# Stick-breaking attention by adjacent heads in separate PSUM banks, and expert weights laid out in runs of four rows

## The chip, the cores and the metric

The kernel runs on one core of a Trainium2 chip. The metric is the device time of one execution in microseconds (us); every execution starts with all weights in HBM, and 425 MB are read from there in the course of it. The core's engines work side by side, each through its own list of instructions in order: TensorE (PE), VectorE (DVE), ScalarE (ACT), GpSimd (POOL), and SyncE (SP), whose queue issues nearly all transfers. They wait for each other by semaphores.

## The reference

A sequence of 256 tokens of width 1024 goes through a first block of two layers (feed-forward, a mixer with three branches, feed-forward) and a second block (a gated delta rule, attention in a sliding window, a mixture of experts). Two parts matter here. The first is a branch of the mixer, stick-breaking attention with 16 heads of 64 features; `strict` lets a query see only earlier keys:

```python
def _stick_breaking(qc, kc, vc):          # per block of 128 queries
    z = jnp.einsum('bqhd,bkhd->bhqk', qblk, k).astype(jnp.float32) * scale
    strict = kpos[None, :] < qp[:, None]
    log_stay = jnp.where(strict, jax.nn.log_sigmoid(-z), 0.0)
    after = lax.cumsum(log_stay, axis=3, reverse=True) - log_stay
    a = jnp.where(strict, jnp.exp(jax.nn.log_sigmoid(z) + after), 0.0)
    return jnp.einsum('bhqk,bkhd->bqhd', a.astype(v.dtype), v)
```

The second is the mixture of 32 experts, each with a gate and an up matrix of 1024x256 and a down matrix of 256x1024:

```python
    for e in range(N_EXPERTS):
        hid = jax.nn.silu(t @ w_gate[e]) * (t @ w_up[e])
        out = out + combine[:, e:e + 1] * (hid @ w_down[e]).astype(jnp.float32)
```

## The kernel before

Weights are streamed. A tile of 512 KB is loaded on SP's queue (`raw`, four buffers), split into a rounded half `hi` by ACT (L255) and a rest `lo` by DVE (L256), and used by PE in three passes (L250 to L252, or L293, L294 and L296 with the tokens on the partitions). The rest of the mixer is written as generators, and after each weight tile `execute` advances every active one by a step. So PE's list has attention work between the matmuls of weight tiles, in an order that is fixed when the program is built.

Stick-breaking is one such generator, `stick`. `pipe` runs eight units through three stages; in each round it calls s2 of the unit before, then s1 of the newest, then s3 of the one two back (order 1, 0, 2), and then lets three weight tiles go by.

- s1 computes scores. A unit has two heads. Keys lie on the partitions, queries on the columns. Bank A holds keys 0 to 127 against all 256 queries for both heads (two times 256 columns), bank B keys 128 to 255 against queries 128 to 255 (two times 128). A product contracts 64 features, so it uses 64 of the array's 128 rows. In the kernel before both heads of a unit lie on the same half of the partitions (`p`, by `t % 2`), and the mask is added on PE, as a product of the identity and a bf16 mask (L974, L981). ACT takes Abs, Exp and Ln (L985 to L990), DVE makes softplus and log-sigmoid from that (L992, L993) and splits the softplus (`sph` at L995, `spl` at L996).
- s2 forms the running sums by products with a triangular matrix (L1004 for B, L1007 for A, and L1009 for B's part of A); DVE adds them (L1011), ACT takes Exp (L1012).
- s3 multiplies by the values (L1026, L1027). The output has 64 features of a head on the partitions; here both heads of a unit go to the same half of them.

These matmuls have fp32 operands; each of them leaves two records in the trace. `bank` gives one of five PSUM banks (L107) and `sc` a scratch tile of a pool.

The experts run in 16 pairs and one more unit for tokens that overflow. `hidden` multiplies a pair's tokens by gate and up (L1983), with the two experts on the two halves of the output's partitions, in one bank; `down` multiplies by w_down (L2025), `scatter` puts tokens back (L2038). `expert_gu` loads gate and up: two tiles of 1 MB, each with four of the eight blocks of rows, by four transfers of 512 KB on SP (L1784). Partition p takes rows 8p to 8p+7. The tiles come from a pool of 14 buffers. `expert_d` loads w_down in two tiles (L1798) into the pool of five that `lo` uses. SP issues them in order, and each waits for its buffer and for an earlier transfer.

Of the kernel before, what the change touches and what calls it, by code (L numbers as in the profile page):

```python
# [7 lines left out]
F32 = mybir.dt.float32  # L8
F32R = mybir.dt.float32r
BF16 = mybir.dt.bfloat16  # L10
I32 = mybir.dt.int32
AF = mybir.ActivationFunctionType
ALU = mybir.AluOpType
# [4 lines left out]
S = 256  # L18
NB = 2
KD = 8  # L20
# [69 lines left out]
class Net:  # L90
# [873 lines left out]
    def stick(self, L):  # L964
        nc = self.nc
        nu, none = self.NU[:, 0:128], self.NU[:, 128:129].to_broadcast([128, 128])
        P = {}
        flat = lambda a: a.rearrange("p a b -> p (a b)")

        def s1(t):  # L970
            qT, kT = L["qc"], L["kc"]
            p = slice(64 * (t % 2), 64 * (t % 2) + 64)
            A, B = self.bank([128, 2, S]), self.bank([128, 2, 128])
            nc.tensor.matmul(B, self.identb, self.m_str.rearrange("p (o n) -> p o n", o=1).to_broadcast([128, 2, 128]), start=True, stop=False)  # L974
            for i in range(2):
                r = 2 * (t // 2) + i
                nc.tensor.matmul(B[:, i, :], kT[p, r, 128:256], qT[p, r, 128:256], start=False, stop=i == 1)
            for i in range(2):
                r = 2 * (t // 2) + i
                nc.tensor.matmul(A[:, i, :], kT[p, r, 0:128], qT[p, r, :], start=i == 0, stop=False)  # L980
            nc.tensor.matmul(A[:, :, 0:128], self.identb, self.m_str.rearrange("p (o n) -> p o n", o=1).to_broadcast([128, 2, 128]), start=False, stop=True)  # L981
            for nm, z in (("B", flat(B)), ("A", flat(A))):
                n = z.shape[1]
                e = self.sc([128, n], F32, "ze")
                nc.scalar.activation(e, z, AF.Abs)  # L985
                if t == 0 and nm == "B":

                    self.tc.keep_in_program_order(nc.scalar.preload_act_table_set("natural_log_exp_and_others"))
                nc.scalar.activation(e, e, AF.Exp, scale=-1.0)
                nc.scalar.activation(e, e, AF.Ln, bias=1.0)  # L990
                sp = self.sc([128, n], F32, "sp", True)
                nc.vector.scalar_tensor_tensor(sp, z, 0.0, e, op0=ALU.max, op1=ALU.add)  # L992
                nc.vector.scalar_tensor_tensor(e, z, 0.0, e, op0=ALU.min, op1=ALU.subtract)  # L993
                hi, lo = self.sc([128, n], F32R, "sph"), self.sc([128, n], F32R, "spl")
                nc.vector.tensor_copy(hi, sp)  # L995
                nc.vector.tensor_tensor(lo, sp, hi.bitcast(F32), op=ALU.subtract)  # L996
                P[nm, t] = (e, hi, lo)

        def s2(t):
            eB, *spB = P["B", t]  # L1000
            eA, *spA = P["A", t]
            B = self.bank([128, 256])
            for i, s in enumerate(spB):
                nc.tensor.matmul(B, nu, s, start=i == 0, stop=i == 1)  # L1004
            A = self.bank([128, 2, S])
            for i, s in enumerate(spA):
                nc.tensor.matmul(flat(A), nu, s, start=i == 0, stop=False)  # L1007
            for i, s in enumerate(spB):
                nc.tensor.matmul(A[:, :, 128:256], none, s.rearrange("p (a b) -> p a b", a=2), start=False, stop=i == 1)  # L1009
            for e, x in ((eB, B), (eA, flat(A))):  # L1010
                nc.vector.tensor_tensor(e, e, x, op=ALU.add)  # L1011
                nc.scalar.activation(e, e, AF.Exp)  # L1012

        def s3(t):
            if t == 0:
                L["stick"] = (self.t8([128, KD, S], F32R, "och"), self.t8([128, KD, S], F32R, "ocl"))
            if t % 2 == 0:
                P["o"] = self.bank([128, 2, S])
            v = L["vc"]
            aB, aA = P.pop(("B", t))[0], P.pop(("A", t))[0]  # L1020
            p = slice(64 * (t % 2), 64 * (t % 2) + 64)
            for i in range(2):
                h = 4 * (t // 2) + t % 2 + 2 * i
                o = P["o"][p, i, :]
                hc = slice(h * 64, h * 64 + 64)
                nc.tensor.matmul(o, v[:, 0, hc], aA[:, i * 256:(i + 1) * 256], start=True, stop=False)  # L1026
                nc.tensor.matmul(o[:, 128:256], v[:, 1, hc], aB[:, i * 128:(i + 1) * 128], start=False, stop=True)  # L1027
            if t % 2 == 1:
                oh, ol = L["stick"]
                r = t - 1  # L1030
                self.split(oh[:, r:r + 2, :], ol[:, r:r + 2, :], P["o"])

        yield from self.pipe(8, (s1, s2, s3), 3, order=(1, 0, 2),
                             ready=lambda t: all((n, min(t, 7) // 2) in L["done"] for n in ("qc", "kc")) and (t < 2 or ("vc", min(t - 2, 7) // 4) in L["done"]))

# [742 lines left out]
    def expert_gu(self, e):  # L1778
        nc, I = self.nc, self.I
        ts = []  # L1780
        for j in range(2):
            t = self.big.tile([128, 2048], F32, name="wgu", tag="b8").rearrange("p (k s n) -> p k s n", k=4, s=2)
            for s, nm in ((0, "w_gate_2"), (1, "w_up_2")):
                nc.sync.dma_start(t[:, :, s, :], I[nm][0, e].rearrange("(p k) n -> p k n", k=KD)[:, 4 * j:4 * j + 4, :])  # L1784
            ts.append(t)
        return lambda k: [(slice(0, 512), ts[k // 4][:, k % 4, :, :].rearrange("p s n -> p (s n)"))]

    def expert_d(self, e, big=False, later=None):
        src = self.I["w_down_2"][0, e].rearrange("(p k) n -> p k n", k=2)
# [515 lines left out]
```

## Time and profile before

| | |
|---|---|
| runs | 2177.97, 2170.87, 2175.85 us; median 2175.85 |
| profiled execution | 2174.99 us, span 2173.1 us |
| PE busy | 2113.4 us, 97% of the span |
| DVE busy | 1342.6 us, 62% |
| ACT busy | 994.7 us, 46% |
| POOL busy | 83.3 us, 4% |
| HBM read | 425.50 MB, 196 GB/s over the span |

The span is the time from the first to the last instruction of one profiled execution, and busy means that an engine had an instruction under way. Stick-breaking runs from about 250 to 350 us in layer 0 and from about 1090 to 1190 us in layer 1; the experts run from about 1890 us to the end. The page's rows show one execution; the median above is over others.

### The profile page before, as it was taken

Reading aid. Unit: us, or ns where it says so; the run is one execution under the profiler, and the core shown is the slowest. Engines: PE = TensorE matmul, PEld = TensorE weight load, DVE = VectorE, ACT = ScalarE, POOL = GpSimd, SP = SyncE. Lnnn points to the kernel's source line nnn. Section 1 sums busy time; section 2 is a strip of 40 time slices with the busy share of each in tenths; the row PEclk is TensorE's granted clock in tenths of the full one; section 3 lists DMA queues with packets and bytes.
Section 4 is the critical chain, followed back from the end, with each engine's and each line's share of the span. In section 5 each row is a group of like instructions: output and inputs, shape, how many; then the busy total and the mean of one; then the engine's idle time right before and its main releaser. Section 6 shows DMA issues by size and latency. Waiting matters only on the chain.

```text
span 2173.1 us, 35223 instructions
## 1 busy us (share of the span) xinstructions
PE 2113.4 (97%) x14059; PEld 1805.8 (83%) x14059; DVE 1342.6 (62%) x2289; ACT 994.7 (46%) x1671; POOL 83.3 (4%) x73
## 2 busy tenths in 40 slices
PE   8999999999999999999999999999999999798998
PEld 8997978899999988998888889998997888544543
DVE  5556567966676567666677884676555885622232
ACT  5443564765444443444465665544443654211111
POOL 0000000100000000000000010000000111101000
PEclk9999999999999999999999999999999999899999
DMA  7575543455467786887543454465675423799996
GB/s 237 179 213 178 167 115 116 149 156 153 144 193 236 231 274 209 267 266 266 168 131 106 135 161 150 147 187 171 185 224 155 142 81 119 261 347 332 354 344 248
DMA packets 316983, 428.91 MB, mean 197 GB/s; under 512 B 20782, under 2 KB 262672, under 8 KB 315792
## 3 DMA queue, kind: packets, MB, share of 16 engines
q1 hardware_dynamic: 316384, 423.48, 62.3%
q0 software_dynamic: 432, 3.15, 0.3%
q8 instruction: 112, 1.84, 0.3%
q14 instruction: 55, 0.45, 0.1%
HBM read 425.50 MB, written 1.07 MB: 196 GB/s over the span
## 4 chain that ended last, share of the span: by engine, by line
PE 85%; DVE 7%; DMA 4%; ACT 2%; issue 1%; POOL 0%; SPq 0%; ACTq 0%; DVEq 0%; POOLq 0%
PE ps L250 14%; PE ps L252 14%; PE ps L251 14%; PE ps L1983 5%; PE y L293 4%; PE y L294 4%; PE ps L293 3%; PE y L296 3%; PE ps L296 3%; PE ps L294 3%; PE ps L2025 3%; DMA raw<-in_w_ada_dram 2%; DVE lo L256 2%; PE y L2038 1%; PE ps L2130 1%; PE y L282 1%
## 5 line engine op out<-in xcount | busy, mean ns | idle before, releaser
L256 DVE TENSOR_TENSOR lo<-raw,hi 128x1024 fp32r<-128x1024 f32 (+1 forms) x556 | 661.2, 1194 | 437.8 <-ACT hi L255 436.5
L255 ACT CAST hi<-raw 128x1024 fp32r<-128x1024 f32 (+1 forms) x556 | 569.3, 1029 | 697.9 <-PE ps L251 245.4
L250 PE MATMUL ps<-xh,hi 128*128 128x256 f32 (+1 forms) x2232 | 635.3, 285 | 0.0
L252 PE MATMUL ps<-xh,lo 128*128 128x256 f32 (+1 forms) x2232 | 632.0, 283 | 2.2 <-DVE lo L256 2.2
L251 PE MATMUL ps<-xl,hi 128*128 128x256 f32 (+1 forms) x2232 | 631.5, 283 | 0.0
L252 PEld LDWEIGHTS ps<-xh,lo 128*128 128x128 f32 (+1 forms) x2232 | 425.6, 191 | 3.0 <-DVE lo L256 2.4
L250 PEld LDWEIGHTS ps<-xh,hi 128*128 128x128 f32 (+1 forms) x2232 | 425.8, 191 | 2.4 <-issue 1.6
L251 PEld LDWEIGHTS ps<-xl,hi 128*128 128x128 f32 (+1 forms) x2232 | 425.8, 191 | 0.7
L293 PE MATMUL ps<-hi,xh 128*128 128x512 f32 (+1 forms) x368 | 145.8, 397 | 1.2 <-ACT xh L255 0.7
L296 PE MATMUL ps<-hi,xl 128*128 128x512 f32 (+1 forms) x368 | 143.9, 391 | 0.3
L294 PE MATMUL ps<-lo,xh 128*128 128x512 f32 (+1 forms) x368 | 143.7, 391 | 0.0
L293 PE MATMUL y<-hi,hh 128*128 128x512 f32 x352 | 137.5, 391 | 0.0
L294 PE MATMUL y<-lo,hh 128*128 128x512 f32 x352 | 137.2, 390 | 0.2
L1983 PE MATMUL ps<-wgu,hi 128*64 128x512 f32 x512 | 123.9, 598 | 0.0
L296 PE MATMUL y<-hi,hl 128*128 128x512 f32 x352 | 104.5, 389 | 0.0
L1983 PEld LDWEIGHTS ps<-wgu,hi 128*64 128x64 f32 x512 | 42.3, 138 | 70.1 <-issue 67.7
L1124 DVE SCALAR_TENSOR_TENSOR macc<-raw,cols,macc 128x1024 f32<-128x1024 f32 x42 | 53.9, 1282 | 51.7 <-DMA raw<-in_w_ada_dram 51.6
L293 PEld LDWEIGHTS ps<-hi,xh 128*128 128x128 f32 x368 | 69.7, 189 | 17.9 <-issue 2.0
L296 PEld LDWEIGHTS ps<-hi,xl 128*128 128x128 f32 x368 | 69.6, 189 | 16.4 <-DVE xl L256 2.3
L294 PEld LDWEIGHTS ps<-lo,xh 128*128 128x128 f32 x368 | 69.7, 189 | 13.1
L294 PEld LDWEIGHTS y<-lo,hh 128*128 128x128 f32 x352 | 66.1, 188 | 14.4 <-DVE lo L256 1.1
L293 PEld LDWEIGHTS y<-hi,hh 128*128 128x128 f32 x352 | 66.1, 188 | 14.2 <-issue 0.8
(601 smaller groups left out, 3207.8 us busy)
## 6 DMA issues: line engine op xcount, KB each, us to landing
raw<-in_w_mix_in_dram SPq DMA_DIRECT2D x184, 512.0 KB, 3.6
raw<-in_ffn_w_in_dram SPq DMA_DIRECT2D x176, 512.0 KB, 4.6
raw<-in_ffn_w_out_dram SPq DMA_DIRECT2D x88, 512.0 KB, 4.3
wgu<-in_w_gate_dram SPq DMA_DIRECT2D x64, 512.0 KB, 9.2
wgu<-in_w_up_dram SPq DMA_DIRECT2D x64, 512.0 KB, 9.5
lo<-in_w_down_dram SPq DMA_DIRECT2D x54, 512.0 KB, 8.3
raw<-in_w_branch_dram SPq DMA_DIRECT2D x48, 512.0 KB, 3.4
raw<-in_w_ada_dram SPq DMA_DIRECT2D x48, 512.0 KB, 5.0
```

Of the source, the lines that this page charges most:

```text
L250: mm(out, ah, bh, start=start, stop=False)
L251: mm(out, ah, bl, start=False, stop=False)
L252: mm(out, al, bh, start=False, stop=stop)
L255: self.nc.scalar.copy(hi, src)
L256: self.nc.vector.tensor_tensor(lo, src, hi.bitcast(F32), op=ALU.subtract)
L282: self.nc.tensor.transpose(pt[:, k, :], src[:, k * 128:(k + 1) * 128], self.ident)
L293: mm(y, ah[:, t], wh[:, c], start=start, stop=False)
L294: mm(y, ah[:, t], wl[:, c], start=False, stop=False)
L296: mm(y, al[:, t], wh[:, c], start=False, stop=stop)
L1124: nc.vector.scalar_tensor_tensor(acc, raw, c, acc, op0=ALU.mult, op1=ALU.add)
L1983: mm(gu[64 * e:64 * e + 64, c], u["x"](k)[:, 64 * e:64 * e + 64], w, start=k == 0 and i == 0, stop=k == KD - 1 and i == len(ws[0]) - 1)
L2025: mm(y[64 * e:64 * e + 64, :], u["hT"][:, k, 64 * e:64 * e + 64], wd[k][:, c], start=k == 0, stop=k == 1)
```

## The change

In `stick` a unit now has heads 2t and 2t+1, which lie on the two halves of the partitions of feature block t. Each head has a bank of its own, `Z[i]`, with A's scores in columns 0 to 255 (`cA`) and B's in 256 to 383 (`cB`), and the four score products alternate between the heads (L979). The mask is added by DVE in PSUM, once for each head (L984). Abs is taken once for each head and part; the loading of ACT's table follows it. A goes before B from there on, and DVE's softplus and log-sigmoid (L997, L998) are done for each head apart. In s3 the two heads go to the two halves of the output's partitions, products alternating (L1029, L1031). s2 is as before, at L1009 (B), L1012 (A), L1014 (B into A) and L1016.

In `expert_gu` the four rows of a matrix that a partition takes in one transfer now lie beside each other in the tile, so that the transfer is 128x1024 rather than 128x4x256; the operand of `hidden` is then two runs of 256 columns. `expert_d` is as before, at L1802, and the product with w_down at L2029.

```diff
@@ -966,35 +966,40 @@
         nu, none = self.NU[:, 0:128], self.NU[:, 128:129].to_broadcast([128, 128])
         P = {}
         flat = lambda a: a.rearrange("p a b -> p (a b)")
+        halves = [slice(64 * i, 64 * i + 64) for i in range(2)]
+        cA, cB = slice(0, 256), slice(256, 384)
+        strict = self.m_str.rearrange("p (o n) -> p o n", o=1).to_broadcast([128, 2, 128])
         def s1(t):
             qT, kT = L["qc"], L["kc"]
-            p = slice(64 * (t % 2), 64 * (t % 2) + 64)
-            A, B = self.bank([128, 2, S]), self.bank([128, 2, 128])
-            nc.tensor.matmul(B, self.identb, self.m_str.rearrange("p (o n) -> p o n", o=1).to_broadcast([128, 2, 128]), start=True, stop=False)
+            Z = [self.bank([128, 512]) for _ in range(2)]
+            for c, k, q in ((cA, slice(0, 128), slice(0, 256)), (cB, slice(128, 256), slice(128, 256))):
+                for i, p in enumerate(halves):
+                    nc.tensor.matmul(Z[i][:, c], kT[p, t, k], qT[p, t, q], start=True, stop=True)
+            e = {"A": self.sc([128, 2, S], F32, "ze"), "B": self.sc([128, 2, 128], F32, "ze")}
             for i in range(2):
-                r = 2 * (t // 2) + i
-                nc.tensor.matmul(B[:, i, :], kT[p, r, 128:256], qT[p, r, 128:256], start=False, stop=i == 1)
-            for i in range(2):
-                r = 2 * (t // 2) + i
-                nc.tensor.matmul(A[:, i, :], kT[p, r, 0:128], qT[p, r, :], start=i == 0, stop=False)
-            nc.tensor.matmul(A[:, :, 0:128], self.identb, self.m_str.rearrange("p (o n) -> p o n", o=1).to_broadcast([128, 2, 128]), start=False, stop=True)
-            for nm, z in (("B", flat(B)), ("A", flat(A))):
-                n = z.shape[1]
-                e = self.sc([128, n], F32, "ze")
-                nc.scalar.activation(e, z, AF.Abs)
-                if t == 0 and nm == "B":
-                    self.tc.keep_in_program_order(nc.scalar.preload_act_table_set("natural_log_exp_and_others"))
-                nc.scalar.activation(e, e, AF.Exp, scale=-1.0)
-                nc.scalar.activation(e, e, AF.Ln, bias=1.0)
-                sp = self.sc([128, n], F32, "sp", True)
-                nc.vector.scalar_tensor_tensor(sp, z, 0.0, e, op0=ALU.max, op1=ALU.add)
-                nc.vector.scalar_tensor_tensor(e, z, 0.0, e, op0=ALU.min, op1=ALU.subtract)
-                hi, lo = self.sc([128, n], F32R, "sph"), self.sc([128, n], F32R, "spl")
-                nc.vector.tensor_copy(hi, sp)
-                nc.vector.tensor_tensor(lo, sp, hi.bitcast(F32), op=ALU.subtract)
-                P[nm, t] = (e, hi, lo)
+                d = Z[i].rearrange("p (a b) -> p a b", a=2)[:, :, 0:128]
+                nc.vector.tensor_tensor(d, d, strict, op=ALU.add)
+                for nm, c in (("A", cA), ("B", cB)):
+                    nc.scalar.activation(e[nm][:, i, :], Z[i][:, c], AF.Abs)
+            if t == 0:
+                self.tc.keep_in_program_order(nc.scalar.preload_act_table_set("natural_log_exp_and_others"))
+            for nm, c in (("A", cA), ("B", cB)):
+                n = c.stop - c.start
+                x = flat(e[nm])
+                nc.scalar.activation(x, x, AF.Exp, scale=-1.0)
+                nc.scalar.activation(x, x, AF.Ln, bias=1.0)
+                sp = self.sc([128, 2, n], F32, "sp", True)
+                for i in range(2):
+                    nc.vector.scalar_tensor_tensor(sp[:, i, :], Z[i][:, c], 0.0, e[nm][:, i, :], op0=ALU.max, op1=ALU.add)
+                    nc.vector.scalar_tensor_tensor(e[nm][:, i, :], Z[i][:, c], 0.0, e[nm][:, i, :], op0=ALU.min, op1=ALU.subtract)
+                hi, lo = self.sc([128, 2 * n], F32R, "sph"), self.sc([128, 2 * n], F32R, "spl")
+                nc.vector.tensor_copy(hi, flat(sp))
+                nc.vector.tensor_tensor(lo, flat(sp), hi.bitcast(F32), op=ALU.subtract)
+                P[nm, t] = (x, hi, lo)
         def s2(t):
             eB, *spB = P["B", t]
@@ -1018,13 +1023,12 @@
                 P["o"] = self.bank([128, 2, S])
             v = L["vc"]
             aB, aA = P.pop(("B", t))[0], P.pop(("A", t))[0]
-            p = slice(64 * (t % 2), 64 * (t % 2) + 64)
-            for i in range(2):
-                h = 4 * (t // 2) + t % 2 + 2 * i
-                o = P["o"][p, i, :]
-                hc = slice(h * 64, h * 64 + 64)
-                nc.tensor.matmul(o, v[:, 0, hc], aA[:, i * 256:(i + 1) * 256], start=True, stop=False)
-                nc.tensor.matmul(o[:, 128:256], v[:, 1, hc], aB[:, i * 128:(i + 1) * 128], start=False, stop=True)
+            o = P["o"][:, t % 2, :]
+            hc = [slice(128 * t + 64 * i, 128 * t + 64 * i + 64) for i in range(2)]
+            for i, p in enumerate(halves):
+                nc.tensor.matmul(o[p, :], v[:, 0, hc[i]], aA[:, i * 256:(i + 1) * 256], start=True, stop=False)
+            for i, p in enumerate(halves):
+                nc.tensor.matmul(o[p, 128:256], v[:, 1, hc[i]], aB[:, i * 128:(i + 1) * 128], start=False, stop=True)
             if t % 2 == 1:
                 oh, ol = L["stick"]
                 r = t - 1
@@ -1779,11 +1783,11 @@
         nc, I = self.nc, self.I
         ts = []
         for j in range(2):
-            t = self.big.tile([128, 2048], F32, name="wgu", tag="b8").rearrange("p (k s n) -> p k s n", k=4, s=2)
+            t = self.big.tile([128, 2048], F32, name="wgu", tag="b8").rearrange("p (s k n) -> p s k n", k=4, s=2)
             for s, nm in ((0, "w_gate_2"), (1, "w_up_2")):
-                nc.sync.dma_start(t[:, :, s, :], I[nm][0, e].rearrange("(p k) n -> p k n", k=KD)[:, 4 * j:4 * j + 4, :])
+                nc.sync.dma_start(t[:, s, :, :], I[nm][0, e].rearrange("(p k) n -> p k n", k=KD)[:, 4 * j:4 * j + 4, :])
             ts.append(t)
-        return lambda k: [(slice(0, 512), ts[k // 4][:, k % 4, :, :].rearrange("p s n -> p (s n)"))]
+        return lambda k: [(slice(0, 512), ts[k // 4][:, :, k % 4, :])]
     def expert_d(self, e, big=False, later=None):
         src = self.I["w_down_2"][0, e].rearrange("(p k) n -> p k n", k=2)
```

PE, a round of the stick units of layer 0 between the matmuls of weight tiles, in the kernel before (`sph` and `spl` are the halves of the softplus, NU the triangular matrix, bmask the mask, qc and kc queries and keys, ze the attention weights, vc the values):

```order
L1007 MATMUL y<-sph,NU 128x512
L1007 MATMUL y<-spl,NU 128x512
L1009 MATMUL y<-sph,NU 128x2x128
L1009 MATMUL y<-spl,NU 128x2x128
L974 LDWEIGHTS bmask
L974 MATMUL y<-bmask 128x256
L977 MATMUL y<-qc,kc 128x128 x2
L980 MATMUL y<-qc,kc 128x256 x2
L981 LDWEIGHTS bmask
L981 MATMUL y<-bmask 128x2x128
L1026 MATMUL y<-ze,vc 64x256
L1027 MATMUL y<-ze,vc 64x128
```

The same round in the changed kernel:

```order
L1009 MATMUL y<-sph,NU 128x256
L1012 MATMUL y<-sph,NU 128x512
L1012 MATMUL y<-spl,NU 128x512
L1014 MATMUL y<-sph,NU 128x2x128
L979 MATMUL y<-qc,kc 128x256 x2
L1009 MATMUL y<-spl,NU 128x256
L1014 MATMUL y<-spl,NU 128x2x128
L979 MATMUL y<-qc,kc 128x128 x2
L1029 MATMUL y<-ze,vc 64x256 x2
L1031 MATMUL y<-ze,vc 64x128 x2
L296 MATMUL ps<-hi,xl 128x512
```

The two mask products are gone, the heads' products stand two by two, and the second halves of two running sums (`spl`, L1009 and L1014) have moved in between the scores of 256 and of 128 columns.

DVE, one unit's softplus and what stands between, in the kernel before (`lo<-raw,hi` is the split of a weight tile, y a PSUM bank):

```order
L256 TENSOR_TENSOR lo<-raw,hi 128x1024
L992 SCALAR_TENSOR_TENSOR sp<-y,ze 128x256
L993 SCALAR_TENSOR_TENSOR ze<-y,ze 128x256
L995 CAST sph<-sp 128x256
L992 SCALAR_TENSOR_TENSOR sp<-y,ze 128x512
L996 TENSOR_TENSOR spl<-sp,sph 128x256
L993 SCALAR_TENSOR_TENSOR ze<-y,ze 128x512
L995 CAST sph<-sp 128x512
L256 TENSOR_TENSOR lo<-raw,hi 128x1024
L996 TENSOR_TENSOR spl<-sp,sph 128x512
```

The same place in the changed kernel:

```order
L984 TENSOR_TENSOR y<-y,bmask 128x2x128 x2
L997 SCALAR_TENSOR_TENSOR sp<-y,ze 128x256 x2
L998 SCALAR_TENSOR_TENSOR ze<-y,ze 128x256 x2
L1000 CAST sph<-sp 128x512
L997 SCALAR_TENSOR_TENSOR sp<-y,ze 128x128
L1001 TENSOR_TENSOR spl<-sp,sph 128x512
L998 SCALAR_TENSOR_TENSOR ze<-y,ze 128x128
L997 SCALAR_TENSOR_TENSOR sp<-y,ze 128x128
L256 TENSOR_TENSOR lo<-raw,hi 128x1024
L998 SCALAR_TENSOR_TENSOR ze<-y,ze 128x128
L1000 CAST sph<-sp 128x256
L256 TENSOR_TENSOR lo<-raw,hi 128x1024
```

Two mask additions come first, the part of 512 columns goes before the part of 256, and the operations from PSUM have half the columns each and are twice as many.

## Rows read from the trace of the kernel before

**Rows 1.** Page, part 1: engine, busy us, share of span, instructions.

```profile
PE 2113.4 (97%) x14059; PEld 1805.8 (83%) x14059; DVE 1342.6 (62%) x2289; ACT 994.7 (46%) x1671; POOL 83.3 (4%) x73
```

**Rows 2.** Page, part 4: the chain's shares by engine.

```profile
PE 85%; DVE 7%; DMA 4%; ACT 2%; issue 1%; POOL 0%; SPq 0%; ACTq 0%; DVEq 0%; POOLq 0%
```

**Rows 3.** Windows of six stick units, layer 0: sums of busy us, means per unit.

```profile
sum 75.50, PE 75.50 PEld 60.72 DVE 53.33 ACT 44.44 POOL 0.00; mean PE 12.58 PEld 10.12 DVE 8.89 ACT 7.41 POOL 0.00
```

**Rows 4.** Windows, experts: length, busy us (instructions), clock, DMA share, GB/s.

```profile
1897.50:1985.50 88.00, 82.14 (x405) 40.49 (x404) 24.32 (x46) 13.69 (x36) 6.13 (x4) 1.00 1.04 350
...
1990.00:2150.00 160.00, 160.00 (x780) 77.56 (x776) 48.77 (x87) 27.29 (x69) 2.80 (x2) 1.00 1.03 353
```

**Rows 5.** PE timeline, experts: start, us, line, operands, count, idle before, releaser.

```profile
1976.42 0.39 PE L2038 MATMUL y<-yl,PT 128*128 128x512 f32 x1
...
1984.24 1.08 PE L2025 MATMUL ps<-lo,hT 128*64 128x512 f32 x4 [3.98 <-DMA lo<-in_w_down_dram]
...
1989.37 1.88 PE L1983 MATMUL ps<-wgu,hi 128*64 128x512 f32 x7
```

**Rows 6.** PE timeline, one stick unit.

```profile
295.39 0.28 PE L1009 MATMUL y<-sph,NU 128*128 128x256 f32 x1
...
295.63 0.28 PE L974 MATMUL y<-bmask 128*128 128x256 bf16 x1
295.85 0.71 PE L977 MATMUL y<-qc,kc 64*128 64x128 f32 x4
...
297.56 0.65 PE L1026 MATMUL y<-ze,vc 128*64 128x256 f32 x2
...
298.27 0.59 PE L1026 MATMUL y<-ze,vc 128*64 128x256 f32 x2
298.70 0.38 PE L1027 MATMUL y<-ze,vc 128*64 128x128 f32 x2
299.01 1.09 PE L282 MATMUL y<-ctab,qs 128*128 128x128 f32 x8
```

**Rows 7.** PE timeline, scores of the differential attention between weight records.

```profile
364.90 0.39 PE L296 MATMUL ps<-hi,xl 128*128 128x512 f32 x1
365.12 0.39 PE L293 MATMUL ps<-hi,xh 128*128 128x512 f32 x1
365.44 0.92 PE L753 MATMUL y<-ka,qa 64*128 64x256 f32 x8
366.30 0.50 PE L294 MATMUL ps<-lo,xh 128*128 128x512 f32 x1
366.63 0.40 PE L296 MATMUL ps<-hi,xl 128*128 128x512 f32 x1
```

**Rows 8.** Chain of waits, experts: start, us, what, records.

```profile
1949.91 6.87 PE ps L1983 x32
...
2003.79 3.58 PE ps L2025 x16
```

**Rows 9.** Lines by form, stick stage, DVE then ACT: busy us, mean ns, idle.

```profile
L992 DVE SCALAR_TENSOR_TENSOR sp<-y,ze 128x512 f32<-128x512 f32 x8 | 5.5, 687 | 0.4
...
L992 DVE SCALAR_TENSOR_TENSOR sp<-y,ze 128x256 f32<-128x256 f32 x8 | 3.4, 425 | 7.2 <-ACT ze L990 7.2
...
L1011 DVE TENSOR_TENSOR ze<-ze,y 128x256 f32<-128x256 f32 x8 | 3.3, 418 | 3.3 <-PE y L1004 3.3
...
L726 DVE TENSOR_TENSOR ra<-ps,rope_t 128x128 f32<-128x128 f32 x6 | 1.7, 285 | 1.7 <-ACT qs L719 1.6
...
L985 ACT ACTIVATE ze<-y 128x256 f32<-128x256 f32 x8 | 3.1, 383 | 1.3 <-PE y L977 1.2
```

**Rows 10.** Windows, differential attention, 380 to 460 in four: sums and means.

```profile
sum 80.00, PE 79.14 PEld 70.04 DVE 72.24 ACT 57.32 POOL 10.40; mean PE 19.78 PEld 17.51 DVE 18.06 ACT 14.33 POOL 2.60
```

**Rows 11.** DMA packets, 1910 to 1930 us, then 2118 to 2124 us.

```profile
DMA packets 6680, 7.04 MB, mean 352 GB/s; under 512 B 215, under 2 KB 6550, under 8 KB 6678
...
DMA packets 741, 2.46 MB, mean 410 GB/s; under 512 B 73, under 2 KB 216, under 8 KB 701
```

## The prediction

> **What bounds the kernel now.** First the page's busy line and its chain of waits: TensorE (PE) is busy 97% of the span and carries 85% of the chain [rows 1, 2]. So the time moves by what PE does and by the few places where PE waits; VectorE (DVE), ScalarE and the transfers count only where they make PE late. Then the two stretches that the change touches, stage by stage.
>
> In the stick-breaking stage of layer 0 I cut six units of the pipeline apart and asked for busy times: 75.50 us, PE busy 75.50, DVE 53.33 (71%), ScalarE 44.44 [rows 3]. PE does not wait at all there, so what is taken off PE is gained until another engine takes over; DVE has 3.7 us a unit to spare (12.58 less 8.89). Layer 1 has the same eight units again: 16 in all.
>
> In the stage of the experts PE is busy 82.14 of 88 us while the 16 DMA engines are full (share 1.04) and bring 350 GB/s; then, from 1990 on, it is busy all the time [rows 4]. The PE timeline shows where the missing time lies: waits for w_down tiles, the longest of 3.98 us before 1984.24 [rows 5].
>
> **Scores (s1).** Before, a unit starts at 295.63 with a mask matmul and ends at 297.56 with the first of the value products: 1.93 us [rows 6]. Its four fp32 products of 64 rows each leave two records (x4 for two), all on one half of the array, one behind the other. The changed unit keeps four products of the same shapes, but alternates between the halves and puts each head in a bank of its own. That is what the differential attention does already at L753, with two products of 256 and two of 128 columns: the block goes from 365.44 to 366.30, 0.86 us for eight records [rows 7]. Around it the step into the block is 0.32 instead of the 0.22 or 0.23 between weight records (+0.09), and the step behind it 0.33 (+0.10): 1.05 us with both. So s1 saves 1.93 - 1.05 = 0.88 us; the two bf16 mask matmuls are in that. The bounds: nothing beyond the masks and their way out (two records like the one from 295.63 to 295.85, so 0.44, if the halves took turns), and 1.07 if the steps in and out cost nothing. I take the 0.88, since L753 is the same work.
>
> **Value products (s3).** From 297.56 to 299.01: 1.45 us for four fp32 products into one column half of the output [rows 6]. Now the two heads go to the two column halves of one bank. No row of this stage shows that; the nearest is the expert product L1983, whose two experts go to the column halves of one bank: 32 records of 512 columns take 6.87 us, 0.215 each [rows 8], as long as a record of half the columns takes alone at L1026 (0.22, from 298.27 to 298.70 for two). So there the halves run together. Bounds: nothing saved (they run in turn), and all halved (0.72). I take 0.63, half less the steps in and out.
>
> Sum: 16 x (0.88 + 0.63) = 24.2 us. In three of eight units per layer the new order puts the second part of two running sums between the pair of 256 and the pair of 128 columns; that is one more way out of the halves and back, 6 x 0.19 = 1.1 us. It leaves 23.0.
>
> **What DVE and ScalarE pay.** Two additions of the mask in PSUM, 128x256 each, at about the 0.418 us of L1011: 0.84. The four scalar_tensor_tensor become eight: 4 x 0.425 + 4 x 0.285 = 2.84 where they were 2 x 0.687 + 2 x 0.425 = 2.22, so 0.62 more (the 0.285 is L726, another operation of 128x128 from PSUM) [rows 9]. DVE rises by 1.46 to 10.35 us in a unit that PE would do in 12.58 - 1.44 = 11.14: 93%. ScalarE does four Abs instead of two; at the 0.383 of the one of 256 columns two more are at most 0.77 [rows 9], and 7.41 + 0.77 of 11.14 us are covered by PE. A stage with DVE at such a load is in the trace: 80 us of the differential attention with DVE at 72.24 (90%) and PE at 79.14, a loss of 1.1% [rows 10]. On 16 x 11.1 = 178 us this is 2.0, and I take 2.5 since 93 is more than 90. Stick-breaking then gains 20.5 us.
>
> At nothing I put: the table load, which moves behind the Abs's and hides behind PE; the two banks now held until B's last DVE operation, since the next unit needs two of five a period later; and the second operand of L1983 in two runs of 256 (the running sum L1009 reads two runs of 128, and its record lasts 0.28 like that of the mask matmul at 295.63, which PE reads in one repeated run [rows 6]). If the last is wrong by 5%, it is 0.05 x 6.87 = 0.34 us for each of 17 units of the experts, 6 us.
>
> **The experts' loads.** The order of the transfers on the SP queue is the same; each gate and up tile goes in runs of 4 KB instead of 1 KB. While these loads run alone nearly all packets lie between 512 B and 2 KB, and 352 GB/s are moved; in a stretch in which most lie between 2 and 8 KB it is 410 GB/s [rows 11]. The 88 us at 350 GB/s are 30.8 MB; two thirds of that are gate and up. At 410 they would take 75 us, and what landed at 1985.5 would land by 1973, before PE asks for it at 1976.65. What goes is the wait: from 1976.65 (the last L2038 and its 0.23) to 1989.37 lie 12.7 us [rows 5], in which PE does 16 records of L2025, 3.58 us where nothing is late, and three of L1983, 0.64 [rows 8]; 8.5 us are lost. At a rate between the two a part stays; the ends are 0 and 8.5, and I take 8, the nearest row being the 410. Next late would be PE itself, as from 1990 on.
>
> **Sum.** 2174.99 (the profiled execution; its span is 2173.1) - 20.5 - 8.0 = 2146.5. The median of the runs is 0.9 above that execution, so the forecast is 2147.
>
> **Rivals.**
> (a) The loads come no faster, since 350 is what this core gets in that stretch whatever the run: 2174.99 - 20.5 = 2154.5, on the scale of the medians 2155. For it: the rate is flat, 350 to 353, over 260 us. Against: the 410 in the same stage. The Trainium skill, page "DMA: Bandwidth & Descriptors", section "Specifications", speaks for this one: it gives about 358 GB/s as the limit of HBM for a core and 512 B as enough for line rate, by which runs of 1 KB lose nothing and the time would be the 2155 of this case rather than 2147. The measured 410 differs from it, which is why the case gets no more than 0.15.
> (b) DVE's chain gets longer than PE's period. On PE the spl half of the running sum stands ahead of the second score pair, the value products and the weight matmuls; all of them wait if spl is late, and spl now stands behind two masks, eight operations and up to two splits of weight tiles. At 1 us a unit instead of 2.5 in all: 2174.99 - 23.0 + 16 - 8 = 2160, or 2161.
> (c) Slower: the same wait at 3 us a unit, when each unit's chain through ScalarE and DVE no longer fits between two visits: 2174.99 - 23.0 + 48 - 8 = 2192, or 2193. It decides from 2.3 us a unit on, where (31 + 6.5)/16 are used up. Against it: DVE has 0.8 us a unit left, and PE waits for DVE nowhere in [rows 3].
> (d) The column halves of s3 run in turn, against [rows 8]: 10.1 us less gain, 2157.
>
> **How the numbers follow.** Forecast 0.58, (a) 0.15, (b) 0.16, (c) 0.06, (d) 0.05. The forecast's own range is 2139 to 2155: down to both pairs exactly halved and no loss by DVE (16 x (1.07 + 0.73) = 28.8, and 8.5: 2139), up to a loss of 6 by DVE and half the gain of the loads (2155). With (a), (d) and most of (b) the range is 2134 to 2166. About 0.3% (6.5 us) is what a measurement can tell: faster means below 2169.3. That holds for the forecast, (a), (d) and nearly all of (b): 0.88; (b) at its worst or (c) at its mildest end within 0.3%: 0.06; the rest of (c) is slower: 0.06.
>
> **What would show it.** Right: the records of L979 start in pairs a few ns apart and a unit's s1 takes about 1.0 us, s3 about 0.8; the mask additions take about 0.42 on DVE; no wait of PE for w_down at the product of L2025 (L2029 now) near 1960; about 400 GB/s while the experts load. Wrong: waits of PE at the running sums with DVE's spl as releaser, a DVE without gaps in the stick units, or the load rate still at 350 with the same waits.

## The result, and the profile after

The changed kernel takes 2144.44 us (median of four runs, 2141.81 to 2146.97), the kernel before 2173.82 in the same comparison: a ratio of 0.9863, interval 0.9841 to 0.9885. That is 29.4 us less. The forecast was 2147, 29 us below the median of 2175.85 that it started from. The page of the changed kernel, the busy line and the shares of the chain, which answer to [rows 1, 2]:

```profile
PE 2089.1 (97%) x14027; PEld 1788.1 (83%) x14027; DVE 1352.7 (63%) x2385; ACT 995.2 (46%) x1703; POOL 84.6 (4%) x73
...
PE 85%; DVE 7%; DMA 4%; ACT 2%; issue 1%; POOL 0%; SPq 0%; DVEq 0%; ACTq 0%; POOLq 0%
```

PE is still the bound. To see where the time came from I measure two stages in each trace: stick-breaking in a layer, from the first score product to the first of the differential attention (L753), and the experts, from the small product that PE does after the routing (L1903 before, L1907 after) to the end of the span.

| us | stick, layer 0 | stick, layer 1 | experts | time |
|---|---|---|---|---|
| before | 120.12 | 120.08 | 286.13 | 2174.99 |
| changed | 109.74 | 109.75 | 277.17 | 2146.97 |
| difference | -10.38 | -10.33 | -8.96 | -28.02 |

The last column is that of the profiled executions. So stick-breaking gave 20.7 us (20.5 was forecast) and the experts 9.0 (8.0). Together the stages gained 29.7 us, 1.7 more than the 28.0 by which these two executions differ; the 1.7 lie in parts that neither edit touches, and those vary: the first stage alone starts at 245.05 to 246.34 us in the kernels below.

One stick unit on PE in the changed kernel (start, us, line, operands, count), against [rows 6]:

```profile
294.00 0.28 PE L1014 MATMUL y<-sph,NU 128*128 128x256 f32 x1
294.12 0.28 PE L1014 MATMUL y<-spl,NU 128*128 128x256 f32 x1
294.33 0.92 PE L979 MATMUL y<-qc,kc 64*128 64x256 f32 x8
295.18 0.65 PE L1029 MATMUL y<-ze,vc 128*64 128x256 f32 x4
295.67 0.39 PE L1031 MATMUL y<-ze,vc 128*64 128x128 f32 x4
295.98 0.44 PE L282 MATMUL y<-ctab,qs 128*128 128x128 f32 x2
```

The count x8 or x4 holds both heads: their records start in pairs, 7 ns apart. s1 goes from 294.33 to 295.18, 0.85 us, as L753 did [rows 7]; s3 takes 0.80 (to 295.98) instead of 1.45. The step from the last L1014 (294.12) into the halves is 0.21 where it is 0.12 between the two L1014. In three units of a layer the running sums stand between the score pairs, and each way back is paid again:

```profile
270.05 0.28 PE L1014 MATMUL y<-sph,NU 128*128 128x256 f32 x1
270.26 0.70 PE L979 MATMUL y<-qc,kc 64*128 64x256 f32 x4
270.89 0.38 PE L1009 MATMUL y<-spl,NU 128*128 128x256 f32 x1
271.11 0.28 PE L1014 MATMUL y<-spl,NU 128*128 128x256 f32 x1
271.32 0.49 PE L979 MATMUL y<-qc,kc 64*128 64x128 f32 x4
271.74 0.65 PE L1029 MATMUL y<-ze,vc 128*64 128x256 f32 x4
```

The windows of the changed kernel: layer 0's stick stage, then the first 88 us of the experts' loads, which answer to [rows 4] (length, busy us of PE, PEld, DVE, ACT, POOL, clock, DMA share, GB/s):

```profile
246.30:352.00 105.70, 105.70 (x625) 86.52 (x626) 87.14 (x214) 67.91 (x131) 0.00 (x0) 1.00 0.44 132
...
1878.50:1966.50 88.00, 87.84 (x438) 43.76 (x440) 27.12 (x50) 14.86 (x38) 6.12 (x4) 1.00 0.96 364
```

PE does not wait in the stick stage, with DVE at 87 of 105.7 us (82%). The experts' wait for w_down is gone: PE is busy 87.84 of 88 us. From 1919 to 1939 the loads ran at the rate of [rows 11]'s second line:

```profile
DMA packets 2240, 8.18 MB, mean 409 GB/s; under 512 B 248, under 2 KB 248, under 8 KB 2238
```

Over the 88 us it is only 364. In the first 30 us (1880 to 1910) it is 339 to 392 in stretches of 10 us, at a DMA share of 0.98 to 1.01, for a reason that no run shows; from 1950 on the DMA engines are no longer full (share 0.83 in 1950 to 1960), and the longest waits of SP's queue in the 88 us are for buffers that PE gives back (26.9 us in sum for those of w_down).

Of the 9.0 us of the experts only 5.7 are idle time of PE in the kernel before, in three waits for w_down. The longest, of 3.98 us, ends at 1984.24. From 1980 to 1985 the granted clock is 1.00, from 1986 to 1988 it is 0.50, the lower level of 1.2 GHz, and a record of L1983 takes 1.11 us (at 1987.29) that takes 0.62 from 1988.91 on. In the changed kernel the clock is 1.00 throughout the loads.

### The profile page after: what moved, and what is told of

The parts are those of the page before. It is cut to its first block, busy times and chain, and to the rows that moved or that the text cites. A ratio compares the mean times of both kernels' runs of the same rounds, so it can differ in the third digit from the quotient of the medians.

```text
span 2145.2 us, 35265 instructions
## 1 busy us (share of the span) xinstructions
PE 2089.1 (97%) x14027; PEld 1788.1 (83%) x14027; DVE 1352.7 (63%) x2385; ACT 995.2 (46%) x1703; POOL 84.6 (4%) x73
## 3 DMA queue, kind: packets, MB, share of 16 engines
HBM read 425.50 MB, written 1.07 MB: 199 GB/s over the span
## 4 chain that ended last, share of the span: by engine, by line
PE 85%; DVE 7%; DMA 4%; ACT 2%; issue 1%; POOL 0%; SPq 0%; DVEq 0%; ACTq 0%; POOLq 0%
PE ps L250 14%; PE ps L251 14%; PE ps L252 14%; PE ps L1987 6%; PE y L293 4%; PE y L294 4%; PE ps L293 4%; PE ps L296 3%; PE ps L294 3%; PE y L296 3%; PE ps L2029 3%; DMA raw<-in_w_ada_dram 3%; DVE lo L256 2%; PE y L2042 2%; PE ps L2134 1%; PE y L282 1%
```

## Experiments

My theory after the result: the two edits are independent, the halves of the array run together, DVE's added work is hidden, and the loads gain by their rate. "Stage" is the stick stage of layer 0 as in the table.

**Each edit alone.** `gu_only` is the kernel before with the new `expert_gu`; `stick_only` is the changed kernel with the old one.

> The kernel before with the expert tiles in runs of 4 KB alone. Theory (the two parts add up): the three waits for w_down between 1976 and 1986 go, the experts' stage from its first product (L1907 of the changed kernel, 1887 here) to the end is 8.9 us shorter, time about 9 us below the kernel before, a ratio of 0.996. Rival (the wait goes because the mixers end earlier and the loads fall into another phase): time as before, the waits stay.

> The changed stick-breaking alone, expert tiles as before in runs of 1 KB. Theory: 20.3 us less in the two stick stages (10.1 each), the three waits for w_down stay, time about 20 us below the kernel before, a ratio of 0.991. Rival (phase): all of 28 us, with the waits gone.

Measured: `gu_only` 2166.4 us against 2175.61, ratio 0.996, interval 0.9945 to 0.9975; stage 120.11, experts 277.4. `stick_only` 2152.35, ratio 0.9901 (0.9881 to 0.9921); stage 109.72, experts 286.1. So the parts add up, as expected. With the old layout two waits for w_down, 4.1 us together, stand in the timeline of `stick_only` as in [rows 5]; `gu_only` has none:

```profile
1957.00 1.08 PE L2029 MATMUL ps<-lo,hT 128*64 128x512 f32 x4 [2.63 <-DMA lo<-in_w_down_dram]
1959.53 1.98 PE L2029 MATMUL ps<-lo,hT 128*64 128x512 f32 x4 [1.45 <-DMA lo<-in_w_down_dram]
```

**Is it the alternation?** `s3_turn` and `s1_turn` write the products of one head first, then those of the other. From here on most kernels ran once, so that what is read is the stages of the trace and not the time.

```diff
             for i, p in enumerate(halves):
                 nc.tensor.matmul(o[p, :], v[:, 0, hc[i]], ...)
-            for i, p in enumerate(halves):
                 nc.tensor.matmul(o[p, 128:256], v[:, 1, hc[i]], ...)
```

(`s1_turn` exchanges the two loops around L979 in the same way.)

> The changed kernel with the value products head by head (256 and 128 columns of one head, then of the other) instead of alternating. Theory (the gain of s3 is that neighbours in the list go to different column halves): the first pair no longer runs together, only what meets at the border between the heads does; s3 rises from 0.80 to between 1.2 and 1.45 us, the stick stage of a layer by 3 to 5 us. Rival (the gain comes from the new place of the output or from fewer switches, not from running together): s3 stays at 0.80.

> The changed kernel with the scores head by head instead of alternating. Theory: s1 rises from 0.85 to between 1.3 and 1.5 us (the four products alone one behind the other took 1.5 us before, without the masks), a layer's stick stage by 4 to 5 us. Rival (the gain of s1 is the two mask products that left PE): s1 stays at 0.85, the stage as in the changed kernel.

Measured: `s3_turn` has a stage of 109.79, nothing lost; `s1_turn` 111.43. The value products of `s3_turn`, then the scores of two units of `s1_turn`:

```profile
271.21 0.66 PE L1029 MATMUL y<-ze,vc 128*64 128x256 f32 x4
271.70 0.40 PE L1030 MATMUL y<-ze,vc 128*64 128x128 f32 x4
272.02 0.50 PE L296 MATMUL ps<-hi,xl 128*128 128x512 f32 x1
```

```profile
258.65 0.93 PE L979 MATMUL y<-qc,kc 64*128 64x256 f32 x8
259.51 0.50 PE L293 MATMUL ps<-hi,xh 128*128 128x512 f32 x1
...
269.06 0.92 PE L979 MATMUL y<-qc,kc 64*128 64x256 f32 x4
269.91 0.38 PE L1009 MATMUL y<-spl,NU 128*128 128x256 f32 x1
270.13 0.28 PE L1014 MATMUL y<-spl,NU 128*128 128x256 f32 x1
270.34 0.92 PE L979 MATMUL y<-qc,kc 64*128 64x256 f32 x4
```

Both theories were wrong; 109.79 is the number of the rival for `s3_turn`, but the halves do run together. In `s3_turn` the whole block still takes 0.81 us (271.21 to 272.02): the second head's first record starts 13 ns behind the first head's, although the edit puts both products of the first head ahead of it. In `s1_turn` the same holds at 258.65 (eight records, 0.86). Only where running sums on the full array stand between the heads, at 269.06, does each head run alone, 0.85 us each. What makes the halves run together here is thus not that neighbours alternate but that nothing of the full array stands between them. What running together is worth follows from two units of one kernel: 0.86 us for both heads at 258.65, 0.85 for each at 269.06. The rest of s1's gain, 1.93 - 1.70 = 0.23 us a unit, is the masks that left PE, less the steps.

**Steps in and out.** `pin` holds the score products in program order.

```diff
-                    nc.tensor.matmul(Z[i][:, c], kT[p, t, k], qT[p, t, q], start=True, stop=True)
+                    self.tc.keep_in_program_order(nc.tensor.matmul(Z[i][:, c], ...))
```

> The changed kernel with the score products held in program order, so that no running sum stands between the pair of 256 and the pair of 128 columns. Theory (each way out of the halves and back costs 0.2 us, three units of a layer): 0.6 us a layer less, 109.1. Rival: the running sum that now stands ahead makes PE wait for spl, the stage becomes longer than 109.74.

Measured: stage 108.92 in both layers, 0.82 less than the changed kernel; time 2142.23 in its one run. All scores are one block again, and PE does not wait. The 0.82 is a net: from one record's start to the next, scores take 6.83 instead of 7.85 us a layer and running sums 8.55 instead of 8.97, but value products 7.55 instead of 6.98, since in one unit the displaced running sums now stand between those. Over two layers it is 1.6 us, below what runs can tell apart; the stages show it.

**What DVE's work costs.** `mask_pe` adds the masks on PE again, in the new banks; `mask_x2`, `mask_x3` and `mask_x5` repeat the addition on DVE; `mask_early` has three additions in units 0 to 5 only.

```diff
                 d = Z[i].rearrange("p (a b) -> p a b", a=2)[:, :, 0:128]
-                nc.vector.tensor_tensor(d, d, strict, op=ALU.add)
+                for _ in range(3):          # 2, 5; in mask_early 3 if t < 6 else 1
+                    nc.vector.tensor_tensor(d, d, strict, op=ALU.add)
```

In `mask_pe` the line is `nc.tensor.matmul(d, self.identb, strict, start=False, stop=True)` behind the scores.

> The changed kernel with the mask added by PE, one product of identity and mask per bank behind the scores, instead of by DVE. PE gets two bf16 products of 256 columns per unit (0.12 each and one step of 0.1), DVE loses 0.86 us per unit. Theory (DVE costs PE nothing at its load): the stage rises from 109.74 by 1.5 to 3 us. Rival (the 2.5 us that I charged to DVE for both layers are there): the stage stays within 0.8 us, since what DVE gives back pays for part.

> The changed kernel with the mask added three times instead of once in each bank, 4 more DVE operations of 0.428 us per unit, 13.7 us a layer. The stage is measured from the first score product to the first product of the differential attention: 109.74 us in the changed kernel. Theory (DVE's work is hidden while it fits the stage: 87.1 + 13.7 = 100.8 of 105.7): 109.7 to 111.5. Rival (b of the prediction: each added us in the chain before spl makes PE wait): about 123.

> The same with the mask added five times: 27.4 us more DVE work a layer, 114.5 in a stage in which DVE has 105.7. Theory (cover until DVE is full, then DVE is the bound): the stage becomes 118 to 125 us, with PE waiting at the running sums on spl and at weight products on lo. Rival (b): about 137. If it stays below 114 the cover reaches beyond the stage.

> The mask added three times in units 0 to 5 of a layer and once in units 6 and 7. With three times in all units the stage is 123.9 us, 14.1 more, but PE waits only 1.2 us in the first six units; 8.3 us of waiting stand at its end, where the small DVE operations of the state-space branch (L827 to L849) and those of the last two units share DVE, and TensorE's clock falls there. Theory (the edge is the end of the stage): the stage is 110 to 112.5 us, though three quarters of the added work is there (10.3 us). Rival (added DVE work costs PE its own length wherever it stands): 109.74 + 0.75 x 14.1 = 120.

> The mask added twice in all units: 6.85 us more DVE work a layer. In the changed kernel the small operations end (L849) 0.8 us before PE reaches the product that wants them (L853 at 338.35). Theory (edge at the end, 0.8 us of slack there): two units there bring 1.7 us more, PE waits 1 to 3 us, the stage 111 to 114 us. Rival (no cost until DVE's share is above the 95% of the last run): 109.7.

Measured stages, and at which matmul of weight tiles (of the 432 between the first score product and L753) PE's list has the last unit's scores and L853, the first product of the state-space branch that needs DVE's small operations. The DVE work is the lengths of the added records in sum:

| kernel | DVE added, us a layer | stage, us | last scores at | L853 at |
|---|---|---|---|---|
| changed | 0 | 109.74 | 348 | 382 |
| mask_pe | masks gone | 110.02 | 348 | 377 |
| mask_x2 | 6.85 | 117.88 | 359 | 384 |
| mask_early | 10.3 | 122.01 | 381 | 384 |
| mask_x3 | 13.7 | 123.87 | 384 | 384 |
| mask_x5 | 27.4 | 133.24 | 384 | 384 |

Where PE waited in `mask_early`, and its windows up to the end of the stage (columns as above):

```profile
345.20 0.61 PE L853 MATMUL y<-dA,ctab 128*128 128x16 f32 x2 [4.66 <-DVE dA L849]
...
350.05 0.77 PE L293 MATMUL ps<-hi,xh 128*128 128x512 f32 x1 [1.94 <-DVE ra L727]
```

```profile
245.00:335.00 90.00, 89.33 (x532) 72.34 (x531) 74.83 (x169) 57.37 (x110) 0.00 (x0) 1.00 0.47 141
335.00:350.00 15.00, 8.44 (x40) 6.17 (x38) 11.58 (x47) 4.52 (x12) 0.00 (x0) 0.82 0.12 36
350.00:364.00 14.00, 13.95 (x62) 11.04 (x64) 9.92 (x24) 7.02 (x10) 0.00 (x0) 0.82 0.32 87
```

In the changed kernel the same stretch has no wait:

```profile
335.00:350.00 15.00, 15.00 (x82) 12.28 (x81) 13.46 (x42) 7.46 (x12) 0.00 (x0) 1.00 0.30 79
```

All five theories failed (that of `mask_pe` is taken up below), and with them my picture of the cover as a sum of free DVE time. `mask_x3`, in which the work would still fit (100.8 of 105.7), lost 14.1 us; `mask_x2` lost 8.1 for 6.85. And it does not matter in which unit the work is: `mask_early`, with nothing added to the last two units, lost 12.3. Yet PE waits hardly at all in the first 90 us of the stage (0.67 us in `mask_early`). The last two columns of the table show what moved. The order of PE's list is fixed when the program is built; with more DVE work in each unit, the last unit's scores land later in it, up to the place of L853, which hardly moves. In the changed kernel 34 weight matmuls lie between the two; in `mask_early` 3. The running sum of the unit before stands beside those scores, and in DVE's list its addition (L1017 here) stands ahead of most of the 20 or so small operations of the state-space branch (L827 to L849), which follow one another between operations of the last unit. In `mask_early` DVE first waits for PE there:

```profile
339.15 0.42 DVE L1017 TENSOR_TENSOR ze<-ze,y 128x256 f32<-128x256 f32 x1 [1.65 <-PE y L1010]
```

Then PE, which has only the 3 weight matmuls left, waits 4.66 us for L849, and 1.94 for the rope (L727). The granted clock is 1.00 until the first of these waits; from 345 to 352 us it is 0.50 (1.2 GHz), where it was 1.00 in the changed kernel. The 12.3 us are 7.3 of waiting, about 4.0 of the slower clock (an estimate, half of the 8.0 us that PE works at it), and 1.0 by which the other records take longer in the new order. For `mask_x2` the same reckoning gives 3.5, 3.0 and 1.6. That the order of the lists is the cause is argued from the lists and not shown: no kernel keeps the order of the changed one and adds DVE work alone.

The rivals' numbers came nearer than mine (120 for `mask_early`, 123 for `mask_x3`), but for most of the price not for their reason: in layer 0 of `mask_x2`, `mask_x3` and `mask_early` PE waits at the running sums for at most 0.5 us. `mask_x5` lost 23.5, between its theory and its rival; there PE does wait at the running sums, 6.6 of 18.1 us of waiting, for DVE's sph.

`mask_pe` has no wait of PE either, and its stage is 0.28 longer than the changed kernel's. That number would fit my rival as well. But the mask products do take 2.23 us a layer from one record's start to the next, 0.28 a unit, about what the theory took. What hides them is the list: no running sum stands between the score pairs, as in `pin`, and scores and running sums take 1.0 and 0.7 us less than in the changed kernel. So the stage says nothing on DVE either way. What does is that PE waits nowhere in the changed kernel's stage: the 6.85 us of DVE work cost no wait there, and taking them away had none to give back.

**The rate of the loads.** `gu_2k` and `gu_512` are the changed kernel with other layouts of the same tile: pairs of rows, or half rows, lie together. Number and size of the transfers are the same, and in HBM the four rows of a partition lie together in all of them; what differs is the length of the runs in the tile.

```diff
-... .rearrange("p (s k n) -> p s k n", k=4, s=2)
+... .rearrange("p (h s k n) -> p h s k n", h=2, k=2, s=2)      # gu_2k
+... .rearrange("p (k h s n) -> p k h s n", k=4, h=2, s=2)      # gu_512
```

> The changed kernel with gate and up tiles laid out so that a transfer goes in runs of 2 KB. Stage of the experts, from the onehot product (L1907) to the end of the span: 286.1 us before, 277.2 in the changed kernel, 277.3 with that edit alone. Theory (the rate depends on the length of a run, between 350 GB/s at 1 KB and 410 at 4 KB): about 380 GB/s, most of the wait gone, the stage 278 to 281. Rival (only the 4 KB runs, one per partition and matrix, get the higher rate): 286, with the waits for w_down. Rival (the rate has nothing to do with it, the layout of the operand has): 286 or 277, not between, with 350 GB/s.

> The changed kernel with gate and up in runs of 512 B. Theory (rate by run length; taking a fixed part per packet from 48 ns for 1 KB and 165 ns for 4 KB, about 28 ns for 512 B, some 310 GB/s with w_down's runs in it): the loads bound the stage almost throughout, waits for w_down and also for gate and up tiles, the stage 300 to 325 us. Rival (512 B moves at the rate of 1 KB): 286. Rival (the rate has nothing to do with it): 277.

| runs of | kernel | experts, us | GB/s, first 88 us | time, us |
|---|---|---|---|---|
| 512 B | gu_512 | 308.6 | 299 | 2176.03 |
| 1 KB | stick_only | 286.1 | 352 | 2152.35 |
| 2 KB | gu_2k | 277.0 | 360 | 2146.08 |
| 4 KB | changed | 277.2 | 364 | 2144.44 |

The windows of `gu_512` and of `gu_2k`, and the longest wait of `gu_512`:

```profile
1879.00:1967.00 88.00, 84.47 (x400) 40.79 (x396) 24.98 (x51) 14.38 (x36) 6.13 (x4) 0.96 1.07 299
```

```profile
1880.00:1968.00 88.00, 87.86 (x438) 43.48 (x436) 27.66 (x54) 15.69 (x38) 6.13 (x4) 1.00 0.98 360
```

```profile
1974.61 5.23 PE L2029 MATMUL ps<-lo,hT 128*64 128x512 f32 x13 [7.49 <-DMA lo<-in_w_down_dram]
```

At 512 B and 1 KB the DMA engines are full (share 1.07 and 1.04) and PE waits; at 2 and 4 KB they are not full to the end of the 88 us (0.98 and 0.96), PE does not wait for loads, and the queue waits for PE's buffers. So the rate by run length decides, and 2 KB are enough here. That `gu_2k` has the 277 us of the 4 KB runs would also fit the rival by which the operand's layout counts and not the rate; `gu_512`, with 308.6 and 17.1 us of waits for w_down, does not fit it. `gu_2k` against the kernel before is 0.9863 (0.9841 to 0.9885), as the changed kernel is. I had expected a rest of 1 to 4 us with 2 KB; there was none. The 300 to 325 us expected for 512 B were right. With 512 B the whole of the stick gain is lost again: ratio 1.0003 (0.9989 to 1.0018).

## Why the prediction was right

- **s1** (0.88 a unit) and **s3** (0.63, from the experts' column halves): the mechanism is right. Summed from one record's start to the next, the scores, masks and value products of a stage went from 26.6 to 14.8 us a layer, and the first unit's mask product, 0.2, stood ahead of the stage: 24.0 for both layers. The nearest rows, L753 and L1983, were the same work, which is why the size nearly held.
- **The steps in and out**: mis-sized. In such a sum the step into the halves falls on the record ahead, a running sum, and the running sums' records grew from 7.60 to 8.97 us a layer, 2.7 for both. So PE's gain was 24.0 - 2.7 = 21.3 us where the prediction, with the first step of each unit in its 24.2 and 1.1 for the second way, had 23.0. Of the missing 1.7, 0.7 is in the steps (22 of its 0.09 are 2.0, where the running sums show 2.7), and 1.0 in the blocks themselves. Of the 21.3, the 0.4 of the two first mask products lie ahead of the stages.
- **DVE** (2.5 us, by the 90% of [rows 10]): this term failed; it was nothing that a wait of PE shows. Its load came out at 82% and not 93%: the forecast added up the lengths of the records, 1.46 us a unit, but neighbouring records of DVE overlap (at 333.98 one of 0.42 us starts, the next at 334.32), and its busy time rose from 1342.6 to 1352.7 us, 0.63 for each of 16 units. And a loss read from another stage said nothing about this one. The two errors have opposite signs and nearly cancel, which is luck: the stages gained 20.7 where 20.5 was forecast.
- **Rivals (b) and (c)**: in the changed kernel they did not happen, but (b) was near: 0.86 us more DVE work in a unit costs 8.1 us a layer, about 1 us a unit as (b) had it. The place I named, spl at the running sums, is not where it shows first: that is the branch whose small DVE operations come at the end of the stage. Only in `mask_x5` do the running sums wait for more than 0.5 us, and for sph.
- **The loads** (8 us): 9.0. The mechanism is the one forecast. The rate reached 409 where 410 was taken, but not throughout: it was 405 to 413 from 1910 to 1950 and 364 over the 88 us, and the wait went all the same. What the forecast read as 8.5 us of waiting was 5.7 of idle PE; much of the rest was PE's work drawn out, in part by the clock of 0.50 behind the wait, which the prediction did not see. Rival (a) is refuted by the four layouts: 350 GB/s was not what the core gets whatever the run. The page "DMA: Bandwidth & Descriptors" of the Trainium skill (section "Specifications": 512 B is enough for line rate) differs here from 296 GB/s in 20 us of nearly pure 512 B runs (`gu_512`, 1900 to 1920) and 352 at 1 KB [rows 11], both with full engines, against 409 at 4 KB; the measurement decides.
- **Rival (d)**: refuted by 295.18 to 295.98. **Two runs in L1983's operand** at nothing: right, a record of that product takes 596 ns where it took 598.

The quickest kernel of the study, by its stages together, is `pin` (108.92 twice and 277.1). It was run once, at 2142.23, and is not shown to be faster than the changed one (2141.81 to 2146.97).

## What to carry to other kernels

Two products of 64 rows or 64 columns cost about as much as one, if they lie on different halves of the array and nothing of the full array stands between them (0.86 us for both heads' scores, 0.85 for one head's alone). Read the price from a place in the same trace that does it already, and count each way into the halves and out. When loads bound a stage, look at the length of the runs on both sides: here the layout of the tile in SBUF alone was worth 9 us. Records of DVE overlap, so the sum of their lengths is not its load (1.46 us a unit in sum, 0.63 of busy time). And do not read the cover of an added operation from an engine's mean load alone: look for the next place where another branch needs the same engine, and at how far the built order keeps them apart.

## What was not expected of the hardware

The second half's products do not wait for those listed ahead of them on the first half: in `s3_turn` they started 13 ns behind, with both products of the first head (0.8 us together) ahead in the list; alternating, it is 7 ns. And the rate of loads with full engines rises with the run's length beyond 512 B and 1 KB: 296, 352, 395 and 409 GB/s in 20 us each of runs of 512 B (`gu_512`), 1 KB, 2 KB (`gu_2k`, 1920 to 1940) and 4 KB, the longer two with w_down's runs among them.
